# Column scales spread by a stride-0 weight read, modulation prepared later, split work re-ordered, value products in turns

## The chip, the cores and the metric

The kernel runs on one core of one Trainium2 chip. The metric is device time in microseconds (us) of one execution. Three runs of the kernel before took 2587.75, 2595.44 and 2596.06 us; their median is 2595.44 us.

## The reference

Two stacked blocks, each with two layers, on 256 tokens of width 1024, in float32.

```python
# first block, per layer
h = rms_norm(x, norm_mix_pre)
m = sigmoid(ga)*(conv(h)@wa) + sigmoid(gb)*(headnorm(retention(h))*silu(rg) @ wb) \
  + sigmoid(gc)*(headnorm(gated_linear_attention(h))*silu(gr) @ wc)
x = x + rms_norm(m @ w_out, norm_mix_post)
x = x + rms_norm((silu(h2 @ w_gate) * (h2 @ w_up)) @ w_down, norm_ffn_post)   # h2 = rms_norm(x, norm_ffn_pre)

# second block, per layer, for 256 latent tokens and 256 context tokens
mod = silu(c) @ ada_w[l] + ada_b[l]            # shift, scale and gate columns
hx  = rmsnorm(x, norm1_w) * (1 + sc1) + sh1
x   = x + g1 * (merge of conformer_conv, bidirectional mLSTM, attention with 8 heads of 64) @ w_out
x   = x + g2 * conv_ffn(rmsnorm(x, norm2_w) * (1 + sc2) + sh2)
```

`rms_norm` divides each token by the root of its mean square over the 1024 columns; `headnorm` does so in each head. In the attention, the probabilities of 64-column heads multiply values of 64 columns.

## The kernel before, in words

The kernel is bound to weights: 2-D weights stream from memory in chunks of 128x1024 float32 (512 KB), by `load` (L188) on SP's DMA queue, into five `raw` buffers. `halve` splits a chunk into a high half (`whi`, ACT, L197) and a low half (`wlo`, DVE, L199), both in a rounded float32 form that TensorE takes in one pass. Activations are split in the same way (`xh`/`xl`, `hh`/`hl`, `fah`/`fal`). `mmT` then makes 24 matmuls of 256 columns out of a chunk: high times high (L214), high times low (L218), low times high (L220). The other token-major form is L228 to L232; in the very first projection `pk`, lines 655 and 656.

The program is one long stream of such chunks with the other work laid between. A scheduler orders instructions by priority; `high_priority(offset=PRE_...)` pulls a step forward (splits, norms, `soon`), `issue_after` holds one behind another. Side work (scores, norms, convolutions) lies in generators, advanced by `tick()` after each chunk's matmuls.

The pieces that the change touches:

- **Norms.** `squares` (ACT L252, POOL or DVE sums L255/L259), a matmul with a column of ones (`st`, L273), and `rs_pair`: the -1/2 power on POOL (L281). `rs_diags` then scales the identity by the column, one 128x128 tile `dg` for each half of the tokens (DVE, L289), and `spread` (L296) multiplies a matrix of ones by it, which gives the scale on all partitions (`rsb`). `warm` puts spare matmuls into the wait.
- **Modulation.** `ada_prep` loads the two vectors `c`, each spread to 128 partitions (512 KB), on ACT's DMA queue (L357) and makes silu of them with a tanh on ACT (L361) and a DVE operation (L362). `ada_step` (L376) streams one 512 KB chunk of `ada_w` and multiplies it by the two vectors: two custom DVE operations, with sums to `mods`. There are 96 such steps. `ada_pace(every)` says how many weight chunks lie between two steps.
- **Retention and GLA.** `gn_finish` does the head norm: mean (L945, L946), centring (`on`, L947), sum of squares (L953), `rsqrt` (eight small DVE instructions, L239 to L244), scaling. `gla_scores` makes `gs` (PE, L922), and DVE L930 copies it under a mask. `ga` (ACT L860) feeds the matmul `gl` (L866).
- **Attention.** After the scores (`sc`, L1435) and their transposes (`pT`), the value products `po` (L1455) take 64 columns of values as the stationary operand. Two heads write the two 64-partition halves of one accumulator; `r` is the half, `k` the block of 128 keys (four blocks, or two for the context).
- **The end.** `down` (L214 to L220, `dn`) makes output rows in four pairs `j`; after each, `b2_residual` (L1814) adds it to `xc`, and SP writes it out (L1893).

Of the kernel before, what the change touches and what calls it, by code (L numbers as in the profile page):

```python
# [8 lines left out]
F32 = mybir.dt.float32  # L9
# [3 lines left out]
AF = mybir.ActivationFunctionType  # L13
# [89 lines left out]
class Kern:  # L103
# [87 lines left out]
    def halve(self, raw, n, after=None):  # L191

        nc = self.nc
        with self.tc.high_priority(offset=self.PRE_SPLIT):
            hi = self.p_w.tile([128, 1024], F32R, tag="whi", name=self.nm("whi"))[:, 0:n]
            lo = self.p_w.tile([128, 1024], F32R, tag="wlo", name=self.nm("wlo"))[:, 0:n]
            nc.scalar.activation(hi, raw, AF.Copy)  # L197
            with self.tc.issue_after(after.ins) if after else nullcontext():
                self.mark = nc.vector.tensor_tensor(out=lo, in0=raw, in1=hi.bitcast(F32), op=ALU.subtract)  # L199
        return hi, lo  # L200
# [63 lines left out]
    def rs_cols(self, parts, mean_ones):  # L264


        nc = self.nc
        V = nc.vector
        ps = self.aux("st")
        n = parts[0].shape[-1] // 128  # L270
        for i, p in enumerate(parts):
            for tt in range(n):
                self.small = nc.tensor.matmul(ps[:, 2 * tt : 2 * tt + 2], p[:, tt * 128 : (tt + 1) * 128], mean_ones, start=i + tt == 0, stop=i == len(parts) - 1 and tt == n - 1)  # L273
        return self.rs_diags(ps[:, 0 : 2 * n : 2])

    def rs_pair(self, x, scale):

# [3 lines left out]
        self.nc.gpsimd.tensor_tensor(out=y, in0=h, in1=self.mhalf[:, 0:n], op=ALU.pow)  # L281
        return y

    def rs_diags(self, x):

        self.rsy = y = self.rs_pair(x, 1.0)
        dg = [self.dgt() for _ in range(x.shape[-1])]
        for tt in range(len(dg)):
            self.nc.vector.tensor_scalar(dg[tt], self.ident, y[:, tt : tt + 1], None, ALU.mult)  # L289
        return dg  # L290

    def spread(self, dg):

        ps = self.aux("rsb")
        for t in range(len(dg)):
            self.small = self.nc.tensor.matmul(ps[:, t * 128 : (t + 1) * 128], self.ones, dg[t], start=True, stop=True)  # L296
        return ps[:, 0 : 128 * len(dg)]

    def warm(self, n):

# [6 lines left out]
    def setup(self, es):  # L307
# [42 lines left out]
        self.silu = c.tile([128, 2, 1024], F32, name="silu")  # L350
        self.mods = c.tile([128, 2, 48, 2], F32, name="mods")

    def ada_prep(self):
        nc = self.nc
        for s in range(2):
            v = self.silu[:, s]
            nc.scalar.dma_start(v, self.d["c2"][s : s + 1].to_broadcast([128, 1024]))  # L357
            for i in range(2):
                th = self.u("adr")
                x = v[:, 512 * i : 512 * i + 512]  # L360
                nc.scalar.activation(th, x, AF.Tanh, scale=0.5)  # L361
                nc.vector.scalar_tensor_tensor(x, th, 1.0, x, ALU.add, ALU.mult)  # L362

# [122 lines left out]
    def b1_norm(self, wname):  # L486

        A, V = self.nc.scalar, self.nc.vector  # L490
        st = {}
        hl = [(self.u("xh", F32R), self.u("xl", F32R)) for _ in range(4)]
        with self.tc.high_priority(offset=self.PRE_NORM):
            for j, (hi, lo) in enumerate(hl):
                for a in range(2):
                    sl, k = slice(a * 256, a * 256 + 256), 2 * j + a
                    A.activation(hi[:, sl], self.xc[:, k, 0:256], AF.Copy, scale=self.col(wname, k))
        with self.soon():
            for j, (hi, lo) in enumerate(hl):
                for a in range(2):  # L500
                    sl, k = slice(a * 256, a * 256 + 256), 2 * j + a
                    V.scalar_tensor_tensor(lo[:, sl], self.xc[:, k, 0:256], self.col(wname, k), hi[:, sl].bitcast(F32), ALU.mult, ALU.subtract)
        self.later("norm", self.b1_norm_rest(wname, st))
        return (*self.pairs(hl), st)

    def b1_norm_rest(self, wname, st):
        A, V = self.nc.scalar, self.nc.vector
        now = self.now
        yield from self.until(now + 1)
        with self.soon():  # L510
            parts = self.squares([self.x_pair(j) for j in range(4)])
        yield from self.until(now + self.T1)
        with self.tc.high_priority(offset=self.PRE_NORM):
            dg = self.rs_cols(parts, self.m1024)
            st["y"] = self.rsy
        xw = []
        for j in range(4):
            t = self.u("xw")
            for a in range(2):
                A.activation(t[:, a * 256 : a * 256 + 256], self.xc[:, 2 * j + a, 0:256], AF.Copy, scale=self.col(wname, 2 * j + a))  # L520
            xw.append(t)
        yield from self.until(now + self.T2)
# [12 lines left out]
        yield  # L535
# [134 lines left out]
            self.nc.tensor.transpose(ps[0:16, t * 128 : t * 128 + 128], m[t], self.ident)  # L670
        return ps[0:16, 0:256]

    def down(self, l, j, H, L, name):

        ps = self.mm("dn")
        for r, kt in ((0, 8), (8, 8), (16, 6)):
            for a in range(2):
                w = self.chunk(name, l, r * 128, kt, (2 * j + a) * 128, 128)
                self.mmT(ps[:, a * 256 : a * 256 + 256], w, H[r : r + kt], L[r : r + kt], first=r + a == 0, last=r == 16 and a == 1)
                self.tick()  # L680
        return ps
# [9 lines left out]
    def b1_layer(self, l, ahead):  # L691
# [21 lines left out]
        self.later("gla", self.gla_scores(gla))  # L713
        if l == 0:
            self.later("conv", self.b1_tables())
            self.ada_prep()
            for i in range(2):
                for nm in ("ret_gn_w", "gla_gn_w"):
                    c = self.cols(f"{nm}{i}")
                    V.tensor_scalar(c, c, 0.5, None, ALU.mult)  # L720
        else:
            self.ada_pace(8)
        gv.append(self.u("gv"))
        A.activation(gv[1], self.b1_tok(l, GV + 256, H, L), AF.Copy)
        rv = []
# [54 lines left out]
        def branch(b, j, y, gt):  # L780
# [10 lines left out]
            else:  # L791
                (V if b == 2 else G).tensor_tensor(out=macc[j], in0=macc[j], in1=gt, op=ALU.add)

        for j in range(4):
            branch(0, j, yA, gates(0, j))
        gB = [gates(1, j) for j in range(3)]
# [25 lines left out]
        first.append(self.b1_pairT(l, 256, H, L, "w_ffn_gate"))  # L822
        self.drain("norm")
        H, L = st["HL"]
        self.ada_pace(2, 1)
        for j in range(B1_FF // 2):
            pg = first[2 * j] if j < 2 else self.b1_pairT(l, 256 * j, H, L, "w_ffn_gate")
            if j < 2:
# [53 lines left out]
    def gla_scores(self, gla):  # L882
# [11 lines left out]
        for i, h in enumerate(lv):  # L894
            if h is None:
                q, k = gq, gk
            else:
# [2 lines left out]
                c4 = cum.rearrange("p (a n m) -> p (a n) m", a=2, m=2 * h)  # L900
                e4 = e.rearrange("p (a n m) -> p (a n) m", a=2, m=2 * h)
                V.tensor_tensor(out=e4, in0=c4, in1=c4[:, :, h - 1 : h].to_broadcast([128, 2 * n, 2 * h]), op=ALU.subtract)
                V.scalar_tensor_tensor(e, e, -1.0, e, ALU.mult, ALU.min)
                A.activation(e, e, AF.Exp, scale=1.0 / 16)
                q, k = self.u("ql"), self.u("kl")
                V.tensor_tensor(out=q, in0=gq, in1=e, op=ALU.mult)
                G.tensor_tensor(out=k, in0=gk, in1=e, op=ALU.mult)
# [25 lines left out]
    def gn_finish(self, o_tok, wname, sg, center, name, res):  # L933
# [5 lines left out]
        for tt in range(2):  # L939
# [13 lines left out]
            V.tensor_reduce(v, sq.rearrange("p (h v) -> p h v", h=4), AX.X, ALU.add)  # L953
            V.tensor_scalar(v, v, 1.0 / 128, EPS, ALU.mult, ALU.add)
            y = self.sm("rsh", 4)
            self.rsqrt(y, v, 4)
            V.tensor_tensor(out=c3, in0=c3, in1=y[:, :, None].to_broadcast([128, 4, 128]), op=ALU.mult)
            on.append(c)
            yield
# [453 lines left out]
    def attention(self, qT, kv, out, pool, scores):  # L1413
# [4 lines left out]
        for i in range(4):  # L1418
# [30 lines left out]
                turn(*b)  # L1449
                yield  # L1450
            po = self.aux("po")
            for r in range(2):
                for k in range(nk):
                    vt = kv[k // 2][1]
                    T.matmul(po[64 * r : 64 * r + 64, 0:256], vt[:, (k % 2) * 128 + 64 * c : (k % 2) * 128 + 64 * c + 64], pT[r][k // 2][:, (k % 2) * 256 : (k % 2) * 256 + 256], start=k == 0, stop=k == nk - 1)  # L1455
            A.activation(hi, po[:, 0:256], AF.Copy)
# [1 line left out]

    def soon(self):
        return self.tc.high_priority(offset=self.PRE_SOON)  # L1460

    def dgt(self):
        return self.p_s.tile([128, 128], F32, tag="dg", name=self.nm("dg"), bufs=4)

    def mlstm_gates(self, l, s, ps, need_rows):

# [398 lines left out]
    def b2_ffn(self, l):  # L1865
# [21 lines left out]
                self.ffn_conv(l, f, ps, c[-1], views)  # L1887
            act.append(self.hl(self.ffn_gate(*c), "fa", 0.5, self.gu if j < 3 else self.u))
        H, L = self.pairs(act)
        for j in range(4):  # L1890
            ps = self.down(l, j, H, L, "ffn_w_down_2")
            self.b2_residual(l, 0, j, ps, 40)
            self.nc.sync.dma_start(self.d["outT"][256 * j : 256 * j + 256].rearrange("(k p) t -> p k t", p=128), self.x_pair(j))  # L1893

    def b2_ffn_both(self, l, latent, prep, ahead):

# [86 lines left out]
    def b2(self):  # L1983
# [7 lines left out]
            self.b2_prep(1)  # L1991

        if "b1" not in self.parts:
            self.ada_prep()
            self.b2_start()
        self.b2_mixer(0, lambda s: (self.drain("norm"), ahead("x", 0, 1, 0, (2, 4), True)) if s == 0 else ahead("c", 0, 1, 1, (3, 5), True))
# [8 lines left out]
    def run(self, es):  # L2005
        tc, nc = self.tc, self.nc
        self.setup(es)
        with tc.high_priority(offset=5000):

            nc.scalar.activation(self.sm("warm", 2), self.m1024, AF.Copy)  # L2010
        if "b1" in self.parts:
# [129 lines left out]
```

## Time and profile before

| | |
|---|---|
| median of three runs | 2595.44 us |
| profiled execution, its time | 2584.17 us |
| profiled execution, its span (first to last instruction) | 2581.5 us |
| TensorE busy (PE) | 2524.3 us, 98% |
| weight loads (PEld, beside PE) | 2319.6 us, 90% |
| VectorE (DVE) | 1949.0 us, 75% |
| ScalarE (ACT) | 1282.6 us, 50% |
| GpSimd (POOL) | 144.4 us, 6% |
| mean granted TensorE clock | 0.997 |

The share of an engine is a mean over 2581.5 us; stages differ. In a timeline row the first number is the start, the second the time from the first start to the last end of the merged instructions (xN), and the bracket the idle time ahead of it and what ended it. Two successive instructions of an engine overlap by some 0.08 us in the records, so a row of one lasts longer than it takes in a stream.

### The profile page before, as it was taken

The numbers are of one execution on the slowest core, as the hardware profiler recorded it, in microseconds if no ns is written. First come the engines' busy times: TensorE is split into PE (matmuls) and PEld (weight loads), VectorE is DVE, ScalarE is ACT, GpSimd is POOL, SyncE is SP. The second block draws the span as 40 slices with busy tenths as digits, with TensorE's granted clock in tenths as the row PEclk, the third lists the DMA queues.
The fourth block names the chain that finished last, engine by engine and source line by source line (L and its number), as shares of the span: only waits on it lengthen the run. The fifth ranks groups of instructions, "written<-read, shape, count | busy, mean of one in ns | idle before, by whom it ended". The sixth has DMA issues, their size and how long they took to land. (4 is left out here: it accounts for less than half of the span.)

```text
span 2581.5 us, 44809 instructions
## 1 busy us (share of the span) xinstructions
PE 2524.3 (98%) x18010; PEld 2319.6 (90%) x18010; DVE 1949.0 (75%) x3254; ACT 1282.6 (50%) x2003; POOL 144.4 (6%) x151
## 2 busy tenths in 40 slices
PE   7999999999999999999999999999999999999999
PEld 7999999999999999888977679988889899999999
DVE  6987799699869958876884456975677674966994
ACT  5545544553454546343444534642345644665763
POOL 0100000010100001000010110000000000000000
PEclk9999999999999999999999999999999999999999
DMA  6545488554656754322333224434336333444554
GB/s 232 172 165 180 146 266 258 188 196 149 206 177 212 263 182 168 114 90 90 107 102 111 74 107 148 167 124 141 115 127 203 136 106 121 141 131 155 178 190 148
DMA packets 116209, 405.62 MB, mean 157 GB/s; under 512 B 12817, under 2 KB 16529, under 8 KB 116001
## 3 DMA queue, kind: packets, MB, share of 16 engines
q1 hardware_dynamic: 112880, 397.96, 46.0%
q10 hardware_dynamic: 3120, 4.80, 0.5%
q8 instruction: 141, 2.31, 0.4%
q14 instruction: 68, 0.55, 0.1%
HBM read 401.66 MB, written 1.05 MB: 156 GB/s over the span
## 5 line engine op out<-in xcount | busy, mean ns | idle before, releaser
L199 DVE TENSOR_TENSOR wlo<-raw,whi 128x1024 fp32r<-128x1024 f32 (+3 forms) x674 | 816.0, 1215 | 353.9 <-ACT whi L197 352.2
L197 ACT ACTIVATE whi<-raw 128x1024 fp32r<-128x1024 f32 (+3 forms) x674 | 697.7, 1040 | 591.8 <-PE pj L220 222.3
L214 PE MATMUL pj<-hh,whi 128*128 128x256 f32 (+1 forms) x3120 | 528.8, 311 | 5.5 <-ACT whi L197 4.0
L218 PE MATMUL pj<-hh,wlo 128*128 128x256 f32 (+1 forms) x3120 | 523.5, 309 | 4.3 <-DVE wlo L199 3.7
L214 PEld LDWEIGHTS pj<-hh,whi 128*128 128x128 f32 x3120 | 437.3, 188 | 46.2 <-ACT whi L197 5.2
L218 PEld LDWEIGHTS pj<-hh,wlo 128*128 128x128 f32 x3120 | 435.6, 189 | 43.4 <-DVE wlo L199 8.1
L220 PE MATMUL pj<-hl,whi 128*128 128x256 f32 (+1 forms) x2440 | 389.0, 296 | 0.0
L220 PEld LDWEIGHTS pj<-hl,whi 128*128 128x128 f32 x2440 | 329.6, 188 | 17.5 <-issue 0.3
L376 DVE CUSTOM_DVE_ANT_0 adr<-raw,silu 128x1024 bf16<-128x1024 f32 x192 | 238.1, 1245 | 0.5
L220 PE MATMUL pj<-kc,whi 128*128 128x512 f32 (+1 forms) x680 | 151.8, 344 | 0.0
L1263 DVE SCALAR_TENSOR_TENSOR dw<-z,hw,dw 128x512 f32<-128x512 f32 (+1 forms) x240 | 135.9, 609 | 0.2
L220 PEld LDWEIGHTS pj<-kc,whi 128*128 128x128 f32 x680 | 112.2, 188 | 16.7
L1821 ACT ACTIVATE fc<-pj,vecs 128x256 f32<-128x256 f32 (+1 forms) x78 | 52.0, 667 | 113.9 <-PE pj L220 111.3
L228 PE MATMUL pk<-whi,hh 128*128 128x256 f32 (+1 forms) x512 | 88.0, 291 | 0.0
L1822 DVE SCALAR_TENSOR_TENSOR fc<-pj,vecs,fc 128x255 f32<-128x255 f32 (+1 forms) x78 | 47.4, 609 | 48.7 <-ACT fc L1821 47.9
L230 PE MATMUL pk<-wlo,hh 128*128 128x256 f32 (+1 forms) x512 | 83.7, 283 | 0.0
L218 PE MATMUL dn<-fah,wlo 128*128 128x256 f32 (+1 forms) x440 | 76.5, 301 | 0.9 <-DVE wlo L199 0.9
L214 PE MATMUL dn<-fah,whi 128*128 128x256 f32 (+1 forms) x440 | 76.7, 301 | 0.0
L220 PE MATMUL dn<-fal,whi 128*128 128x256 f32 (+1 forms) x440 | 76.5, 300 | 0.1
L228 PEld LDWEIGHTS pk<-whi,hh 128*128 128x128 f32 x512 | 72.5, 190 | 3.0 <-issue 0.7
L255 POOL TENSOR_TENSOR sq<-sq,sq 128x512 f32<-128x512 f32 x15 | 25.2, 1681 | 855.5 <-ACT sq L252 642.8
L214 PE MATMUL pj<-yh,whi 128*128 128x256 f32 (+1 forms) x384 | 71.5, 313 | 0.0
(432 smaller groups left out, 3686.2 us busy)
## 6 DMA issues: line engine op xcount, KB each, us to landing
raw<-stream SPq DMA_DIRECT2D x620, 512.0 KB, 3.6
raw<-ada_stream SPq DMA_DIRECT2D x96, 512.0 KB, 3.9
raw<-stream SPq DMA_DIRECT2D x36, 384.0 KB, 3.5
raw<-stream SPq DMA_DIRECT2D x11, 408.0 KB, 3.2
raw<-stream SPq DMA_DIRECT2D x6, 272.0 KB, 2.7
xc<-xT SPq DMA_DIRECT2D x2, 512.0 KB, 5.6
xc<-cT ACTq DMA_DIRECT2D x1, 1024.0 KB, 10.9
silu<-c ACTq DMA_DIRECT2D x2, 512.0 KB, 12.6
```

The source lines that it names most:

```text
L197: nc.scalar.activation(hi, raw, AF.Copy)
L199: self.mark = nc.vector.tensor_tensor(out=lo, in0=raw, in1=hi.bitcast(F32), op=ALU.subtract)
L214: mm(out, wh[:, k, cs], xh[k], start=first and k == 0, stop=False)
L218: mm(out, wl[:, k, cs], xh[k], start=False, stop=False)
L220: mm(out, wh[:, k, cs], xl[k], start=False, stop=last and k == kt - 1)
L228: mm(out, xh[k], wh[:, k, :], start=first and k == 0, stop=False)
L230: mm(out, xh[k], wl[:, k, :], start=False, stop=False)
L255: nc.gpsimd.tensor_tensor(out=sqs[0], in0=sqs[0], in1=sq, op=ALU.add)
L376: nc.vector.tensor_tensor_reduce(junk, raw, self.silu[:, s], 0.5, 0.0, ALU.mult, ALU.add, self.mods[:, l, n, s : s + 1])
L1263: V.scalar_tensor_tensor(d, src, w, d, ALU.mult, ALU.add)
L1821: A.activation(v(t), v(ps), AF.Identity, scale=w(1), bias=self.col(f"ffn_conv_b{l}", f + i))
L1822: V.scalar_tensor_tensor(v(t)[..., 1:256], v(ps)[..., 0:255], w(0), v(t)[..., 1:256], ALU.mult, ALU.add)
```

## The change

It does these things, each in the diff below:

- `spread` takes the column itself: one column is read 128 times with step 0 as the stationary operand, and the identity is the moving operand. `rs_diags`, `dg` and its buffers go (36 DVE instructions).
- Six spare matmuls stand at the start of the program.
- The squares of the first norm are issued after the last high split that was made; the low halves of `xc` lose their raised priority.
- The two loads for silu move to SP's queue, between weight chunks; the tanh part moves to just before the branch loop of layer 0's mixer.
- The pace of `ada_step`: none in the projections of mixer 1 (it was every 8 chunks), every 4 in the branch loop of both layers, every 3 in the FFN (it was every 2). Steps by weight chunk: before, 25 at chunks 90 to 138, 8 at 166 to 222 and 15 at 244 to 272; now 9 at 42 to 74, 17 at 91 to 139, 9 at 194 to 226 and 13 at 244 to 280. The 48 steps after that keep their places.
- `gn_finish` takes the -1/2 power on POOL; a minimum on DVE in the GLA decay becomes an absolute value on ACT.
- The value products run through `k` outside and `r` inside.
- The last quarter of the final output is made by halves, each with its own residual and write, the second in two pieces on two queues.

```diff
-            nc.scalar.activation(hi, raw, AF.Copy)
+            self.high = nc.scalar.activation(hi, raw, AF.Copy)
...
-    def spread(self, dg):
+    def spread(self, y):
         ps = self.aux("rsb")
-        for t in range(len(dg)):
-            self.small = self.nc.tensor.matmul(ps[:, t * 128 : (t + 1) * 128], self.ones, dg[t], start=True, stop=True)
-        return ps[:, 0 : 128 * len(dg)]
+        n = y.shape[-1]
+        for t in range(n):
+            self.small = self.nc.tensor.matmul(ps[:, t * 128 : (t + 1) * 128], y[:, t : t + 1].to_broadcast([128, 128]), self.ident, start=True, stop=True)
+        return ps[:, 0 : 128 * n]
...
+    def ada_load(self):
+        for s in range(2):
+            self.nc.sync.dma_start(self.silu[:, s], self.d["c2"][s : s + 1].to_broadcast([128, 1024]))
...
-            nc.scalar.dma_start(v, self.d["c2"][s : s + 1].to_broadcast([128, 1024]))
...
-        with self.soon():
+        with self.soon(), self.tc.issue_after(self.high.ins):
             parts = self.squares([self.x_pair(j) for j in range(4)])
...
-            self.ada_prep()
+            self.ada_load()
...
-        else:
-            self.ada_pace(8)
...
+        if l == 0:
+            self.ada_prep()
+        self.ada_pace(4, 1)
         for j in range(4):
             branch(0, j, yA, gates(0, j))
...
-        self.ada_pace(2, 1)
+        self.ada_pace(3, 1)
...
-                V.scalar_tensor_tensor(e, e, -1.0, e, ALU.mult, ALU.min)
-                A.activation(e, e, AF.Exp, scale=1.0 / 16)
+                A.activation(e, e, AF.Abs)
+                A.activation(e, e, AF.Exp, scale=-1.0 / 16)
...
-            self.rsqrt(y, v, 4)
+            nc.gpsimd.tensor_tensor(out=y, in0=v, in1=self.mhalf[:, 0:4], op=ALU.pow)
...
-            for r in range(2):
-                for k in range(nk):
+            for k in range(nk):
+                for r in range(2):
...
+        def done(a, ps):
+            k = 6 + a
+            for i in range(1 + a):
+                c = slice(256 * i // (1 + a), 256 * (i + 1) // (1 + a))
+                x = self.xc[:, k, c]
+                V.scalar_tensor_tensor(x, ps[:, c], self.mods[:, l, 40 + k, 0:1], x, ALU.mult, ALU.add)
+                (self.nc.scalar if i else self.nc.sync).dma_start(self.d["outT"][128 * k : 128 * k + 128, c], x)
+
+        self.down(l, 3, H, L, "ffn_w_down_2", done)
...
+            ps = self.aux("warm")
+            for _ in range(6):
+                nc.tensor.matmul(ps[:, 0:256], self.ones, self.one256, start=True, stop=True)
```

How the order of the engines moves, at three places. First ACT in the first projections of layer 0, before: `whi` are the splits of successive chunks, `gv` a copy of a projection, `adr` the tanh for silu, `ga` what the GLA decay's matmul waits for.

```order
L416 DMA xc<-cT 128x8x256
L197 ACTIVATE whi_443<-raw_441 128x1024
L197 ACTIVATE whi_488<-raw_486 128x1024
L709 ACTIVATE gv_416<-pk_152,rs_234 128x256
L709 ACTIVATE gv_416<-pk_153,rs_234 128x256
L357 DMA silu<-c 128x1024 x2
L197 ACTIVATE whi_525<-raw_523 128x1024
L361 ACTIVATE adr_422<-silu 128x512
L361 ACTIVATE adr_425<-silu 128x512
L361 ACTIVATE adr_429<-silu 128x512
L361 ACTIVATE adr_432<-silu 128x512
L860 ACTIVATE ga_471<-ga_472 16x256
```

The same place now (line numbers of the changed file, other buffer numbers):

```order
L413 DMA xc<-cT 128x8x256
L197 ACTIVATE whi_434<-raw_432 128x1024
L197 ACTIVATE whi_479<-raw_477 128x1024
L715 ACTIVATE gv_419<-pk_159,rs_241 128x256
L715 ACTIVATE gv_419<-pk_160,rs_241 128x256
L197 ACTIVATE whi_516<-raw_514 128x1024
L867 ACTIVATE ga_462<-ga_463 16x256
L197 ACTIVATE whi_565<-raw_563 128x1024
```

The four `adr` and the two loads are gone from between the split of the eleventh chunk and `ga`; the loads stand on SP's queue now, one ahead of that chunk's predecessor (`raw_477`) and one ahead of the next (`raw_563`).

Second, DVE in mixer 1 where the retention's head norm meets the GLA scores, before: `ro` is the retention's output, `on` its centred copy, `rsh` and `rst` the steps of the root, `gs` the scores, `cy` and `yal` the convolution branch.

```order
L243 SCALAR_TENSOR_TENSOR rst_7232<-rst_7232,var_7228 128x4
L769 TENSOR_TENSOR cy_7139<-pj_7146,cy_7139 128x512
L244 SCALAR_TENSOR_TENSOR rsh_7231<-rst_7232,rsh_7231 128x4
L946 TENSOR_SCALAR mu_7282<-mu_7282 128x4
L199 TENSOR_TENSOR wlo_7411<-raw_7408,whi_7410 128x1024
L242 TENSOR_TENSOR rst_7232<-rsh_7231 128x4
L579 TENSOR_TENSOR yal_7247<-cy_7139,yah_7246 128x512
L243 SCALAR_TENSOR_TENSOR rst_7232<-rst_7232,var_7228 128x4
L947 TENSOR_TENSOR on_7281<-ro_7178,mu_7282 128x512
L244 SCALAR_TENSOR_TENSOR rsh_7231<-rst_7232,rsh_7231 128x4
L930 COPY_PREDICATED S_6271<-Am_125,gs_7305 128x2x128
```

And now:

```order
L952 TENSOR_REDUCE mu_7204<-ro_7111 128x4
L964 TENSOR_TENSOR on_7154<-on_7154,rsh_7164 128x512
L773 TENSOR_TENSOR cy_7072<-pj_7079,cy_7072 128x512
L953 TENSOR_SCALAR mu_7204<-mu_7204 128x4
L199 TENSOR_TENSOR wlo_7317<-raw_7314,whi_7316 128x1024
L575 TENSOR_TENSOR yal_7169<-cy_7072,yah_7168 128x512
L954 TENSOR_TENSOR on_7203<-ro_7111,mu_7204 128x512
L937 COPY_PREDICATED S_6219<-Am_132,gs_7216 128x2x128
```

The small steps are gone, and the scaling of the first half (`on_7154`, L964) now stands ahead of `cy`, the split and the centring of the second half (`on_7203`).

Third, PE at the first value products of the attention, before: `pT` are the transposed probabilities of the two heads, `vt` the values, x2 are two key blocks in one row.

```order
L1455 MATMUL po_15752<-pT_15532,vt_13152 64x256 x2
L1455 MATMUL po_15752<-pT_15533,vt_13120 64x256 x2
L1455 MATMUL po_15752<-pT_15534,vt_13152 64x256 x2
L1455 MATMUL po_15752<-pT_15535,vt_13120 64x256 x2
```

And now:

```order
L218 MATMUL pj_15604<-hh_10909,wlo_15608 128x512
L1462 MATMUL po_15623<-pT_15403,vt_13031 64x256
L1462 MATMUL po_15623<-pT_15405,vt_13031 64x256
L1462 MATMUL po_15623<-pT_15403,vt_13031 64x256
L1462 MATMUL po_15623<-pT_15405,vt_13031 64x256
L1462 MATMUL po_15623<-pT_15404,vt_12999 64x256
L1462 MATMUL po_15623<-pT_15406,vt_12999 64x256
L1462 MATMUL po_15623<-pT_15404,vt_12999 64x256
L1462 MATMUL po_15623<-pT_15406,vt_12999 64x256
```

The eight matmuls of a group are the same; four of one half and then four of the other have become one of each in turn.

## Rows read from the trace of the kernel before

**Rows 1.** The page, busy time of each engine over the span.

```profile
PE 2524.3 (98%) x18010; PEld 2319.6 (90%) x18010; DVE 1949.0 (75%) x3254; ACT 1282.6 (50%) x2003; POOL 144.4 (6%) x151
```

**Rows 2.** The waits of PE: who for whom, us in total, times, longest.

```profile
PE gl L866 <- ACT ga L860: 3.7, 1, 3.7
...
PE rsb L296 <- DVE dg L289: 2.4, 5, 0.5
```

**Rows 3.** Windows: stretch, its length; busy time by engine, clock, DMA share, GB/s.

```profile
46.05:52.50 6.45, 6.45 (x25) 5.61 (x26) 5.97 (x11) 4.54 (x6) 0.00 (x0) 0.51 0.39 129
128.00:160.00 32.00, 31.39 (x272) 30.43 (x270) 30.99 (x72) 14.27 (x19) 1.72 (x3) 1.00 0.38 132
160.00:245.00 85.00, 85.00 (x758) 84.50 (x756) 60.23 (x85) 41.54 (x50) 9.36 (x6) 1.00 0.54 183
305.00:487.00 182.00, 175.47 (x1478) 170.91 (x1477) 156.78 (x209) 81.98 (x99) 1.80 (x1) 1.00 0.76 250
640.00:745.00 105.00, 104.70 (x922) 103.67 (x921) 82.84 (x120) 51.40 (x63) 11.13 (x7) 1.00 0.62 206
783.00:960.00 177.00, 173.80 (x1487) 172.09 (x1486) 145.39 (x202) 91.09 (x120) 3.29 (x3) 1.00 0.69 230
```

**Rows 4.** Timeline of PE, the first products, 7 to 24 us.

```profile
13.12 0.82 PE L655 MATMUL pk<-whi,xh 128*128 128x272 f32 x2 [2.56 <-ACT whi L197]
...
16.50 0.43 PE L656 MATMUL pk<-wlo,xh 128*128 128x272 f32 x1
...
18.49 0.29 PE L656 MATMUL pk<-wlo,xh 128*128 128x272 f32 x1
...
22.79 1.07 PE L218 MATMUL pj<-xh,wlo 128*128 128x256 f32 x8
23.69 0.50 PE L220 MATMUL pj<-xl,whi 128*128 128x256 f32 x3
```

**Rows 5.** Timeline of ACT, 7 to 14 us.

```profile
10.12 2.17 ACT L252 ACTIVATE sq<-xc 128x512 f32<-128x512 f32 x4
```

**Rows 6.** Timeline of ACT and its queue, 29 to 47 us.

```profile
42.54 1.15 ACT L361 ACTIVATE adr<-silu 128x512 f32<-128x512 f32 x2 [9.26 <-DMA silu<-c]
...
45.88 1.04 ACT L197 ACTIVATE whi<-raw 128x1024 fp32r<-128x1024 f32 x1
```

**Rows 7.** Timeline of PE, 46 to 50 us.

```profile
48.02 1.22 PE L228 MATMUL pk<-whi,hh 128*128 128x256 f32 x4
```

**Rows 8.** Timeline of DVE in FFN 0, 384 to 400 us.

```profile
387.28 1.22 DVE L199 TENSOR_TENSOR wlo<-raw,whi 128x1024 fp32r<-128x1024 f32 x1
388.41 1.22 DVE L376 CUSTOM_DVE_ANT_0 adr<-raw,silu 128x1024 bf16<-128x1024 f32 x1
...
389.56 1.22 DVE L199 TENSOR_TENSOR wlo<-raw,whi 128x1024 fp32r<-128x1024 f32 x1
390.70 0.68 DVE L834 TENSOR_TENSOR s<-pj,s 128x512 f32<-128x512 f32 x1
```

**Rows 9.** Timeline of PE, 605 to 616 us.

```profile
608.04 1.10 PE L220 MATMUL pj<-hl,whi 128*128 128x256 f32 x8
...
613.37 2.04 PE L922 MATMUL gs<-ql,kl 64*128 64x128 f32 x8 [2.47 <-DVE rsh L244]
```

**Rows 10.** Timeline of DVE, 609 to 615 us.

```profile
612.54 0.68 DVE L947 TENSOR_TENSOR on<-ro,mu 128x512 f32<-128x512 f32 x1
```

**Rows 11.** Timeline of PE, attention, 1420.5 to 1425.2 us.

```profile
1421.00 2.86 PE L1455 MATMUL po<-pT,vt 128*64 128x256 f32 x16
1423.79 1.14 PE L1435 MATMUL sc<-kT,qT 64*128 64x256 f32 x8
```

**Rows 12.** The same of 1424 to 1500 us, the groups of two key blocks.

```profile
1452.60 1.09 PE L1455 MATMUL po<-pT,vt 128*64 128x256 f32 x8
```

**Rows 13.** Line 1455 over the whole span: the length of one record.

```profile
L1455 PE MATMUL po<-pT,vt x160: 379/379/431, 1421.0 to 2347.5; 128*64 128x256 f32 x160
```

**Rows 14.** Timeline of all engines, 2575 us to the end.

```profile
2577.63 0.88 DVE L1814 SCALAR_TENSOR_TENSOR xc<-dn,mods,xc 128x256 f32<-128x256 f32 x2 [7.68 <-PE dn L220]
```

More of the change, by code (lines that the diff above doesn't have):

```diff
@@ L273, in rs_cols @@
                 self.small = nc.tensor.matmul(ps[:, 2 * tt : 2 * tt + 2], p[:, tt * 128 : (tt + 1) * 128], mean_ones, start=i + tt == 0, stop=i == len(parts) - 1 and tt == n - 1)
-        return self.rs_diags(ps[:, 0 : 2 * n : 2])
+        self.rsy = self.rs_pair(ps[:, 0 : 2 * n : 2], 1.0)
+        return self.rsy
     def rs_pair(self, x, scale):
@@ L282, in rs_pair @@
         return y
[L284 to L290, printed above, removed]
-    def spread(self, dg):
+    def spread(self, y):
         ps = self.aux("rsb")
-        for t in range(len(dg)):
-            self.small = self.nc.tensor.matmul(ps[:, t * 128 : (t + 1) * 128], self.ones, dg[t], start=True, stop=True)
-        return ps[:, 0 : 128 * len(dg)]
+        n = y.shape[-1]
+        for t in range(n):
+            self.small = self.nc.tensor.matmul(ps[:, t * 128 : (t + 1) * 128], y[:, t : t + 1].to_broadcast([128, 128]), self.ident, start=True, stop=True)
+        return ps[:, 0 : 128 * n]
     def warm(self, n):
@@ L355, in ada_prep @@
         for s in range(2):
-            v = self.silu[:, s]
-            nc.scalar.dma_start(v, self.d["c2"][s : s + 1].to_broadcast([128, 1024]))
             for i in range(2):
                 th = self.u("adr")
-                x = v[:, 512 * i : 512 * i + 512]
+                x = self.silu[:, s, 512 * i : 512 * i + 512]
                 nc.scalar.activation(th, x, AF.Tanh, scale=0.5)
@@ L497, in b1_norm @@
                     A.activation(hi[:, sl], self.xc[:, k, 0:256], AF.Copy, scale=self.col(wname, k))
-        with self.soon():
[L499 to L502, printed above, removed]
+        for j, (hi, lo) in enumerate(hl):
+            for a in range(2):
+                sl, k = slice(a * 256, a * 256 + 256), 2 * j + a
+                V.scalar_tensor_tensor(lo[:, sl], self.xc[:, k, 0:256], self.col(wname, k), hi[:, sl].bitcast(F32), ALU.mult, ALU.subtract)
         self.later("norm", self.b1_norm_rest(wname, st))
@@ L509, in b1_norm_rest @@
         yield from self.until(now + 1)
-        with self.soon():
+        with self.soon(), self.tc.issue_after(self.high.ins):
             parts = self.squares([self.x_pair(j) for j in range(4)])
@@ L671, in turned, with down @@
         return ps[0:16, 0:256]
-    def down(self, l, j, H, L, name):
+    def down(self, l, j, H, L, name, done=None):
         ps = self.mm("dn")
+        if done:
+            for a in range(2):
+                p = ps[:, a * 256 : a * 256 + 256]
+                for r, kt in ((0, 8), (8, 8), (16, 6)):
+                    w = self.chunk(name, l, r * 128, kt, (2 * j + a) * 128, 128)
+                    self.mmT(p, w, H[r : r + kt], L[r : r + kt], first=r == 0, last=r == 16)
+                    self.tick()
+                done(a, p)
+            return
         for r, kt in ((0, 8), (8, 8), (16, 6)):
@@ L1460, in soon @@
         return self.tc.high_priority(offset=self.PRE_SOON)
-    def dgt(self):
-        return self.p_s.tile([128, 128], F32, tag="dg", name=self.nm("dg"), bufs=4)
     def mlstm_gates(self, l, s, ps, need_rows):
@@ L1889, in b2_ffn @@
         H, L = self.pairs(act)
-        for j in range(4):
+        for j in range(3):
             ps = self.down(l, j, H, L, "ffn_w_down_2")
@@ L1993, in b2 @@
         if "b1" not in self.parts:
+            self.ada_load()
             self.ada_prep()
```

## The prediction

> **What bounds the kernel now.** I read the page first: PE is busy in 2524.3 of 2581.5 us [rows 1], so no more than 57 us of the span are free of TensorE, and a change that leaves its matmuls as they are can win only from these, from stretches at the lower clock, and from matmuls that run beside each other and do not yet. Then I read the waits of PE: they are small and many; one of 3.7 us for `ga` and, further on, one of 2.5 us for the GLA scores stand out, and five for `dg` make 2.4 us [rows 2, 9]. The windows then show where waits come in a body: in FFN 0 PE misses 6.5 of 182 us, in FFN 1 3.2 of 177, and DVE is busy 157 and 145 us there [rows 3]. The same view shows one stretch at a granted clock of 0.51, which is the 1.2 GHz level, right behind the wait for `ga`.
>
> **The change part by part.** The sum is made against the profiled execution (2584.17 us, of which 2581.5 are span, and 2.7 lie around it); the median of the runs is 11.3 us longer, and I take the same gain off it.
>
> *Spare matmuls, and squares behind the splits.* In the first products PE runs at the lower level: one that lasts 0.43 us in the records at 16.5 lasts 0.29 at 18.5 [rows 4]. PE also waits 2.56 us up to 13.12 for a split, and ACT does four squares from 10.12, for 2.17 us, ahead of it [rows 4, 5]. Behind the splits these 2.2 us go from that wait at most; the spare matmuls can raise the clock early. From 13.1 to 18.4 some 22 products stand about 0.23 us apart instead of 0.125, so 2.3 us can go there. Both together are at most 4.5 us; the chunks still have to arrive and be split, so I take 2.0 (0 to 4.5). If the norm, which now starts 2 us later, ends later, the `xl` products wait for nothing of it; the spread behind it does, and there products stand by to fill.
>
> *Silu later.* The loads are issued on ACT's queue behind the 1 MB of `cT`, and ACT waits 9.26 us for them, to 42.54; `ga` and the split of the next chunk stand behind the waiting instruction, so the split starts at 45.88, with no DMA named: its chunk lay there [rows 6]. PE idles 3.69 us, then does `gl` and gets to the next chunk at 48.02 [rows 2, 7], and 46.05 to 52.5 runs at 0.51 [rows 3]: 6.45 us for what takes 3.3 at the upper level. With the four tanh gone, `ga` follows its own matmul at once. What is late next is the chunk itself: 1 MB of silu now comes ahead of it in SP's queue, which is 4.2 us at the 250 GB/s of FFN 0 [rows 3]; before, the same megabyte ran beside it in another queue, so it is pushed back by less. The rows bound its landing only from above, by 45.9. I put the end of its split at 42 (43 at worst): PE, which runs dry at 42.3 now and will do so at 40, then waits 1 to 2 us instead of 3.7. I take 2.2 for the wait and 3.1 for the clock: 5.3 (1.5 if the clock falls all the same, 6.8 if the whole goes).
>
> *The pace of the modulation.* Between direct neighbours a low split takes 1.13 us of DVE, a custom operation 1.15, an elementwise one 0.60 [rows 8]. Four chunks of the FFN give PE 12 groups of eight matmuls, 0.90 us from one group's start to the next's [rows 4]: 10.8 us. DVE needs 4 x 1.13 for splits, 2 steps x 2 x 1.15, and three elementwise operations: 4.5 + 4.6 + 1.8 = 10.9. So at a step every two chunks DVE has no slack, and each hiccup reaches PE. At a step every three it is 4.5 + 3.1 + 1.8 = 9.4, 86%. Of the 6.5 + 3.2 us of idle PE, each of a dozen waits costs some 0.2 more than its idle time (the last matmul's record runs on), so 12.5 us; I let two thirds go: 8.3. The 9 steps moved to the branch stage need 9 x 2.3 = 20.7 us of DVE; from 160 to 245 it is busy 60.2 of 85 [rows 3], which makes 95%; 128 to 160 is full already (31.0 of 32), and four silu operations (2.4 us) come in at its end, where the head norms' small steps go. In mixer 1 five more steps than before in 640 to 745 make 82.8 + 11.5 of 105, 90%. At 95% I expect a few new waits: -2. So +6.3 for the whole, from -3 to +12.
>
> *Spread without `dg`.* Five waits of `rsb` for `dg` make 2.4 us [rows 2]; two `dg` take some 0.5 us of the chain ahead of each of the 18 spreads, covered by `warm` or side work in the rest. 2.0 (0 to 4). The step-0 read as a weight load is not in these rows for a column; were it slow, 36 loads would each have to be 0.2 us longer to cost 7. I take no cost: loads run beside PE.
>
> *Head norms.* PE's 2.47 us before 613.37 are put down to `rsh`, but the `on` that frees the accumulator ends at 613.2 [rows 9, 10], and that is what counts. In the new order the scaling of the first half, 0.6 us, stands ahead of `cy`, the split and this `on`, against some 0.7 us of small steps that go; so `on` ends where it did and the wait stays. 0.5 for shorter chains later (0 to 6, if the wait and the slow stretch behind it go).
>
> *Value products in turns.* Sixteen records of a group of four key blocks take 2.86 us; eight of two key blocks 1.09 us, eight of `sc`, in two row halves in turns, 1.14 [rows 11, 12]. So twice eight would be 2.0 to 2.2 if the halves ran beside each other throughout; the long group runs one half by itself first. There are eight such groups, so 8 x 0.66 to 0.86: I take 6.7 (less than nothing below). The accumulator's reader, ACT, comes earlier by as much.
>
> The Trainium skill has a rule that speaks against this one ("TensorE: Matmul & The Clock Gate", section "Part 3: Packing small matmuls — row/col tiling"): a weight load runs beside matmuls in flight only when it goes to another row group, and both column halves use all rows. The trace disagrees as far as it goes: eight records of two column halves in 1.09 us are no slower than the row halves' 1.14. By the rule the sum would be that of the rival on the turns below.
>
> *End.* The last pair takes 0.88 us on DVE behind the last matmul [rows 14]; half of it now lies under the last products: 0.4 (0 to 0.6). The absolute value on ACT costs nothing: 16 x 0.6 us on an engine busy half the time.
>
> Sum: 2.0 + 5.3 + 6.3 + 2.0 + 0.5 + 6.7 + 0.4 = 23.2, so 2561 for the profiled execution, and 2595.4 - 23.2 = **2572 us** for the median.
>
> **Rivals.**
> *Waits go whole.* If the scores' wait at 613 goes with its slow stretch (+5.5), the start gives 4.5 and FFN waits go to the last (+5): 2572 - 13 = 2559. For it: DVE has fewer instructions in all. Against: the order at 613.
>
> *Turns don't help.* If no matmul of one half may run beside one of the other, all 16 stand apart as one half's do alone. A record is 0.38 long [rows 13], so the eight of 1.09 us start 0.10 apart in two streams, and one stream's 0.20: 15 x 0.20 + 0.38 = 3.4 us instead of 2.86, so eight groups lose 4.3 where I have +6.7: 2572 + 11 = 2583. For it: the long group now, with only part beside each other. Against it the 1.09 us [rows 12].
>
> *PE's own pace takes it back.* Eight matmuls span 1.07 us at 22.79 and 1.10 at 608 [rows 4, 9]: 4.3 ns a matmul. If the two FFNs without their waits stay at the slower spacing where they had the faster, up to 1478 and 1487 x 4.3 = 6.4 us each are lost [rows 3]; if the chunk at 42 lands late besides, most of the 5.3 goes: 23.2 - 12.8 - 4 = 6: 2589. For it: both spacings stand in the trace; against: they could as well get better.
>
> *Slower: the branch stage overflows.* The 20.7 us of steps meet 24.8 us of DVE that are free from 160 to 245. If the custom operations come in ahead of splits whenever DVE is late, or if the stage needs over 4 us more than I count, the rest falls to PE. Should each of the 18 steps in the two stages hold a split by one operation, 1.15 us, and each third such wait bring a stretch at the lower level (3.2 us, as at 46 to 52 [rows 3]): 18 x 1.15 + 6 x 3.2 = 40, less the 23.2 and the 2 counted: 2610. It decides from 25.2 / 18 = 1.4 us lost a step. Against: the splits have a raised priority, and five buffers lie between.
>
> **How the numbers follow.** Forecast and its neighbourhood (2562 to 2582) 0.58; waits go whole 0.14; turns don't help 0.08; pace takes it back 0.14; overflow 0.06. About 0.3%, 8 us, can be told from no change in this kernel: under 2587.6 is faster. Forecast, first rival, the turns and a third of the pace: 0.85 faster; 0.10 within; 0.05 slower. The likeliest has 2562 to 2582 for its own; the range, 2554 to 2588, leaves out some 0.15 above and 0.04 below.
>
> **What would show it.** Right: no PE wait for `ga`, and clock 1.0 from 46 to 52; FFN 0 with under 3 us of idle PE; groups of `po` at about 2.0 us; no `rsb` wait over 0.3; the scores' wait at about 610 still there. Wrong: DVE over 97% from 160 to 245 with PE waits for `wlo` in it; `po` at 2.9 or more; PE waiting over 3 us for a split near 41; total idle of PE over 50 us.

## The result and the profile after

The changed kernel takes 2551.01 us (median of 4 runs, 2544.71 to 2555.34), the kernel before 2594.94 us (2587.75 to 2596.06): a ratio of 0.9835, 95% interval 0.9803 to 0.9866. That is 43.9 us by the medians and 38.6 us between the two profiled spans (2581.5 and 2542.9). The forecast was 2572 us with a range down to 2554: the right sign, and too little. The page after, against [rows 1]:

```profile
PE 2506.3 (99%) x18022; PEld 2309.3 (91%) x18022; DVE 1921.8 (76%) x3115; ACT 1290.3 (51%) x2017; POOL 155.9 (6%) x159
```

PE has 36.6 us free where it had 57. To see where the time came from, I marked the same points in both traces: the 5416 matmuls that read a low half of a weight chunk come about eight to a chunk, and the n-th stands at the same place of the program.

```
n-th such matmul    before     after    gain so far   stage
    0 (start)          8.1       6.8        1.2
  720 (norm, FFN 0)  310.4     303.9        6.5       first layer's mixer: +5.3
 1200                494.3     478.8       15.5       FFN 0: +9.0
 1440                591.4     575.1       16.3       +0.8
 1560                647.8     624.7       23.1       around the scores of mixer 1: +6.8
 1920                789.4     765.2       24.2       +1.1
 2400                967.4     935.8       31.6       FFN 1: +7.4
 3000               1356.9    1325.9       31.0       -0.6
 3240               1568.4    1533.8       34.6       attention, layer 0: +3.6
 4560               2245.9    2211.2       34.7       0
 4800               2362.7    2325.1       37.7       attention, layer 1: +3.0
 5400               2572.0    2533.6       38.4       +0.7
```

The windows, against [rows 3] (the columns are the same; the stretches are shifted by what was gained):

```profile
39.00:46.00 7.00, 7.00 (x61) 6.22 (x60) 3.55 (x8) 1.42 (x2) 0.00 (x0) 1.00 0.53 198
154.00:239.00 85.00, 85.00 (x758) 84.50 (x756) 76.36 (x95) 42.16 (x51) 13.73 (x8) 1.00 0.68 230
297.00:479.00 182.00, 181.17 (x1525) 180.09 (x1525) 144.38 (x185) 86.63 (x106) 2.00 (x2) 1.00 0.71 237
590.00:600.00 10.00, 9.83 (x81) 9.28 (x80) 8.40 (x16) 4.50 (x7) 1.22 (x2) 1.00 0.17 57
760.00:936.00 176.00, 175.85 (x1526) 174.97 (x1525) 143.19 (x197) 93.46 (x121) 4.85 (x4) 1.00 0.72 235
```

The FFNs have 0.8 and 0.2 us of idle PE where they had 6.5 and 3.2, and the branch stage has none with DVE at 76.4 of 85. The clock is 1.00 behind `ga` and behind the scores. In PE's waits the ones for `ga` and `dg` [rows 2] are gone; the spread now waits for POOL, five times and up to 0.7 us:

```profile
PE pj L218 <- DVE wlo L199: 2.9, 2, 1.7
PE rsb L290 <- POOL rs L282: 2.9, 5, 0.7
...
PE gs L929 <- POOL kl L914: 0.9, 1, 0.9
...
PE gs L929 <- DVE on L954: 0.3, 2, 0.2
```

The timeline of PE at the value products, against [rows 11]:

```profile
1390.07 1.95 PE L1462 MATMUL po<-pT,vt 128*64 128x256 f32 x16
```

Sixteen records take 1.95 us instead of 2.86. At the scores of mixer 1, against [rows 9], and then the end of the program, against [rows 14]. At the end PE has a wait that the kernel before did not have: the second half of the last output rows waits for the residual of the first.

```profile
594.09 1.13 PE L929 MATMUL gs<-ql,kl 64*128 64x128 f32 x8 [0.17 <-DVE on L954]
```

```profile
2531.86 1.17 PE L214 MATMUL dn<-fah,whi 128*128 128x256 f32 x8 [0.67 <-DVE xc L1904]
...
2539.65 0.61 DVE L1904 SCALAR_TENSOR_TENSOR xc<-dn,mods,xc 128x128 f32<-128x128 f32 x2 [7.93 <-PE dn L220]
```

### The profile page after: what moved, and what is told of

Its sections match the earlier page's. It is cut to its first block, busy times and chain, and to the rows that moved or that the text cites. A ratio compares the mean times of both kernels' runs of the same rounds, so it can differ in the third digit from the quotient of the medians.

```text
span 2542.9 us, 44723 instructions
## 1 busy us (share of the span) xinstructions
PE 2506.3 (99%) x18022; PEld 2309.3 (91%) x18022; DVE 1921.8 (76%) x3115; ACT 1290.3 (51%) x2017; POOL 155.9 (6%) x159
## 4 chain that ended last, share of the span: by engine, by line
PE 87%; DVE 8%; ACT 3%; issue 1%; POOL 1%; DMA 0%; ACTq 0%; DVEq 0%; POOLq 0%; SPq 0%
PE pj L214 19%; PE pj L220 19%; PE pj L218 19%; PE dn L220 4%; PE dn L218 4%; PE dn L214 4%; DVE wlo L199 2%; PE pk L228 2%; PE pk L232 2%; PE pk L230 2%; PE pv L1638 2%; DVE dw L1270 1%; PE ms L1598 1%; PE br L214 1%; PE br L218 1%
## 5 line engine op out<-in xcount | busy, mean ns | idle before, releaser
L220 PE MATMUL dn<-fal,whi 128*128 128x256 f32 (+1 forms) x440 | 76.4, 300 | 0.1
```

The lines of the kernel that those rows point to most:

```text
L220: mm(out, wh[:, k, cs], xl[k], start=False, stop=last and k == kt - 1)
```

## The experiments

All spans below are of one profiled execution each. Since they scatter by some 10 us for one and the same kernel (the last experiment but one), the verdicts rest on stages, read between the marks of the table above, and on waits.

**The paces of before in the changed kernel.**

```diff
+        else:
+            self.ada_pace(8)
...
-        self.ada_pace(4, 1)
...
-        self.ada_pace(3, 1)
+        self.ada_pace(2, 1)
```

> The changed kernel with the modulation's paces of the kernel before (every 8 chunks in mixer 1, none of its own in the branch loops, every 2 in the FFNs). Theory: the paces are worth 17 us in the two FFNs and 7 at the scores' wait in mixer 1, so it is 22 to 26 us slower than the changed kernel, with PE idle of some 6 us in FFN 0 and 3 in FFN 1, and a PE wait of about 2 us at the second gs of mixer 1. Rival, that shorter work on DVE elsewhere (norms, head norms) emptied it: 8 us slower at most, and no wait at gs.

Measured: 2563.64 us median (ratio to before 0.989, 0.9856 to 0.9923), span 2554.5, so 11.6 to 12.6 us slower than the changed kernel. FFN 0 takes 182.7 us instead of 174.9, FFN 1 176.4 instead of 170.6, the stretch around the scores 52.4 instead of 49.6, and the start was 3.5 us shorter in this execution. The waits are back, in FFN 0 over 300 to 484 us:

```profile
300.00:484.00 184.00, 177.88 (x1475) 172.59 (x1474) 155.70 (x210) 83.14 (x101) 3.39 (x3) 1.00 0.76 252
```

6.1 us idle and DVE at 156 again, as forecast. The waits come from the paces. Of the 22 to 26 us expected, half showed: the scores got back 2.8 us and not 7 (the next run), the two FFNs 13.6 and not 17, in part because FFN 0 ran with a shorter spacing of PE's matmuls (see the repeated profiles below), and the start was shorter.

**Only mixer 1's pace put back.**

```diff
+        else:
+            self.ada_pace(8)
...
+        if l == 0:
-        self.ada_pace(4, 1)
+            self.ada_pace(4, 1)
```

> The changed kernel with the pace of every 8 chunks put back into mixer 1 alone (the branch loop of layer 1 without a pace of its own). Theory, that one modulation step of 2.3 us on DVE some 20 us ahead made PE wait at the second gs: the wait comes back at 1.5 to 2.5 us with a stretch at the lower clock behind it, 4 to 7 us slower in mixer 1 and nothing elsewhere. Rival, that the head norm's small steps made it (they are still gone here): no wait over 0.5 us, within 1 us of the changed kernel.

Measured: 2549.84 us median, span 2545.6. The stretch around the scores takes 52.4 us instead of 49.6, and PE waits there:

```profile
593.59 1.13 PE L932 MATMUL gs<-ql,kl 64*128 64x128 f32 x8 [1.37 <-DVE on L957]
```

```profile
590.00:600.00 10.00, 8.63 (x56) 8.08 (x56) 8.44 (x16) 4.35 (x7) 1.01 (x1) 0.83 0.21 60
```

The wait (1.37 of 2.47 us) and the lower clock (0.83 in the window) are back by the modulation step alone, with 2.8 of the 6.8 us. That is less than the 4 to 7 us expected; what the head norm's root adds is tested below.

**Only the paces changed in the kernel before.**

```diff
-        else:
-            self.ada_pace(8)
...
+        self.ada_pace(4, 1)
         for j in range(4):
             branch(0, j, yA, gates(0, j))
...
-        self.ada_pace(2, 1)
+        self.ada_pace(3, 1)
```

> The kernel before with the new paces alone (every 4 in both branch loops, every 3 in the FFNs, none in mixer 1's projections). Theory: 22 to 25 us faster than before: 17 in the two FFNs, up to 7 in mixer 1 (a wait of under 1 us at gs, although the small steps of the root are still on DVE), nothing or -1 in the branch loops. Rival, that the branch stage had room only because the other edits emptied DVE: waits of PE for wlo between 160 and 245 us, and 3 to 10 us of the gain lost there.

Measured: 2565.28 us median, ratio to before 0.9899 (0.9865 to 0.9932), span 2559.6: 21.9 us off the span by three changed lines alone. FFN 0 takes 170.7 us (before 183.9), FFN 1 175.3 (178.0), the scores' stretch 50.7 (56.4). The branch stage gives nothing back: at mark 720 it stands 0.8 us ahead of before, and with DVE busy 77.3 of 85 us from 160 to 245 PE has no wait there. Its DVE needs none of the other edits.

**Value products by halves.**

```diff
-            for k in range(nk):
-                for r in range(2):
+            for r in range(2):
+                for k in range(nk):
```

> The changed kernel with the value products half by half again. Theory: groups of sixteen records take 2.86 us again instead of about 1.9, eight groups, so 7 to 8 us slower, all of it in the two attention stages. Rival, that the stages' gain came from the spread of the norms in them: under 2 us slower.

Measured: 2548.96 us median, span 2542.7: by the times, nothing. By the stages, attention takes 211.6 instead of 207.9 us (marks 3000 to 3240) and 117.7 instead of 113.9 (4560 to 4800): 7.5 us slower, as forecast. In this execution the start was 2 us and FFN 0 5.1 us shorter, with not one edit there.

```profile
1382.49 2.86 PE L1462 MATMUL po<-pT,vt 128*64 128x256 f32 x16
```

**The root in small steps on DVE.**

```diff
-            nc.gpsimd.tensor_tensor(out=y, in0=v, in1=self.mhalf[:, 0:4], op=ALU.pow)
+            self.rsqrt(y, v, 4)
```

> The changed kernel with the head norm's root in small steps on DVE again. Theory, that the modulation step made the wait at the second gs of mixer 1: the wait stays under 1 us, the time within 2 us. Rival, that the root on POOL removed it: PE waits 1.5 us or more there, 4 to 7 us slower.

Measured: span 2546.2. Around the scores 51.1 us instead of 49.6; the scores do not wait, a later transpose does, for 1.1 us. The rival is out as the sole cause; the root's steps are worth 1.5 us there.

**Diagonals again.** `rs_diags` and the old `spread` put back, as in the diff of the change.

> The changed kernel with the scaled identities dg again, a matrix of ones as the stationary operand. Theory: the waits of PE at the 18 spreads grow by 0.2 to 0.5 us each where nothing stands by, 2 to 4 us slower in all. Rival, that warm matmuls and side work cover the two dg operations: within 1 us.

Measured: 2540.42 us in its one run, span 2538.5, the shortest of all. Two stages are longer than in kernels with the same spacing of PE's matmuls (see the repeated profiles below): marks 1560 to 1920 take 142.1 us against 140.5 in the changed kernel, and 4560 to 5040 take 201.9 against 199.2 in the next experiment's kernel. In the second, before the last FFN, PE waits for the normed tokens and falls to the lower level for a while:

```profile
2361.42 3.18 PE L214 MATMUL pj<-hh,whi 128*128 128x256 f32 x8 [0.63 <-ACT hh L1146]
```

```profile
2355.00:2375.00 20.00, 19.27 (x135) 17.67 (x135) 18.41 (x36) 15.46 (x35) 0.71 (x1) 0.91 0.32 113
```

The kernel before, which has the diagonals too, waits at the same place:

```profile
2405.35 3.38 PE L214 MATMUL pj<-hh,whi 128*128 128x256 f32 x8 [0.63 <-ACT hh L1133]
```

In the changed kernel the same eight products start without that wait, at a clock of 1.00; from the third on they stand 0.4 us apart here too:

```profile
2367.88 2.60 PE L214 MATMUL pj<-hh,whi 128*128 128x256 f32 x8
```

The first stage is another matter. Its 1.5 us are a stretch at the lower clock among spare matmuls, and the changed kernel, which has no diagonals, has the same stretch at the same place in its second profile; the diagonals' profile first, then that one:

```profile
728.00:743.00 15.00, 13.18 (x83) 11.82 (x82) 9.02 (x16) 8.22 (x17) 3.90 (x3) 0.89 0.30 97
```

```profile
735.00:750.00 15.00, 13.09 (x79) 11.40 (x79) 8.21 (x14) 7.60 (x16) 3.45 (x3) 0.89 0.27 96
```

So the diagonals cost 2.5 to 2.7 us, at one spread and not a little at each of 18; at the others the waits of `rsb` have another name only (2.4 us for `dg`, 2.9 for POOL). The rival, under 1 us, falls, though the time alone would have spoken for it.

**Silu early, on ACT's queue.**

```diff
+            self.ada_prep()
...
-        if l == 0:
-            self.ada_prep()
...
-            self.nc.sync.dma_start(self.silu[:, s]
+            self.nc.scalar.dma_start(self.silu[:, s]
```

> The changed kernel with the silu loads on ACT's queue and the tanh ahead of ga, as before. Theory: PE idles 3 to 4 us at gl again and runs a stretch at the lower clock: 4 to 6 us slower by the time that chunk 30 is reached, nothing later. Rival, that the start's other edits (spare matmuls, squares later) made the gain: under 2 us slower.

Measured: span 2544.4; 6.2 us later at mark 120 (64 us), 4.0 at 250 us. PE waits longer than before and is released at the same instant as in [rows 2, 7]:

```profile
46.06 2.07 PE L872 MATMUL gl<-ga,kc 16*128 16x256 f32 x4 [6.05 <-ACT ga L866]
```

So with silu early the start's other edits buy 2 us that PE then waits.

**The old start.**

```diff
-        with self.soon(), self.tc.issue_after(self.high.ins):
+        with self.soon():
...
-            ps = self.aux("warm")
-            for _ in range(6):
-                nc.tensor.matmul(ps[:, 0:256], self.ones, self.one256, start=True, stop=True)
```

> The changed kernel without the six spare matmuls and with the first squares not held behind the last high split. Theory: the first products run at the lower clock until about 18 us again and PE waits 2 us for a split near 13, 1 to 3 us slower by the time that the first norm's spread is reached, of which some is lost in the wait for a chunk near 41. Rival, that DMA sets the pace up to there: no difference at 50 us.

Measured: span 2547.9; 3.2 us later at mark 30 (26 us), 4.1 at mark 120 and 1.4 at mark 720. The chunk at 41 us did not set the pace, as the rival had it; the difference dies out in the next stage.

**The changed kernel itself, twice more.** No edit.

> The changed kernel itself, unchanged, profiled again. Theory, that the spacing of PE's matmuls (0.113 or 0.118 us) is settled anew in each execution: at least one of FFN 0 and FFN 1 differs by 4 to 5 us from the first profile (FFN 0 174.9 us, FFN 1 170.6 us there between the same matmuls), with as many waits as there. Rival, that the program sets it: both within 0.5 us of the first profile.

> The changed kernel itself, unchanged, profiled a third time; theories and numbers as for the second profile. FFN 0 takes either some 170 or some 175 us, and so does FFN 1; nothing lies between by the theory, unless the spacing changes inside the stage.

Measured: spans 2553.2 and 2552.6 against 2542.9. FFN 0 takes 173.9 in both (174.9 in the first), FFN 1 174.7 in both (170.6), and the end, from mark 5040 to the last mark, 131.7 in both (127.1). PE's waits are nearly the same. The timeline of PE in FFN 1, first the second profile, then the first:

```profile
840.28 1.10 PE L218 MATMUL pj<-hh,wlo 128*128 128x256 f32 x8
841.22 1.10 PE L220 MATMUL pj<-hl,whi 128*128 128x256 f32 x8
```

```profile
840.48 1.07 PE L214 MATMUL pj<-hh,whi 128*128 128x256 f32 x8
841.39 1.07 PE L218 MATMUL pj<-hh,wlo 128*128 128x256 f32 x8
```

Groups of eight start 0.94 or 0.905 us apart. In FFN 1 the first profile has 1265 matmuls spaced about 0.113 us and 170 about 0.118; the other two have 354 and 1071. One and the same program takes either spacing in a stage and mostly keeps it; the 173.9 of FFN 0, between the two lengths that the theory allows, has both inside. FFN 1 and the end make 8.7 of the 10 us between these executions. Stretches at the lower clock add to the scatter: they lie at 11.7 us in the first profile, at 279 and 740 in the second and at 34 and 969 in the third.

The second and third profile agree with each other and come from one chip, so by themselves they do not tell whether the chip or the execution chose. The four runs of the kernel with the value products by halves, all on one chip, took 2544.2, 2544.5, 2553.5 and 2554.0 us: two groups 9 us apart, which speaks for the execution, but no trace shows the spacing of each.

**The rotary tables a projection earlier.** The first remaining waits, between 56 and 72 us.

```diff
             self.b1_masks()
+            self.later("conv", self.b1_tables())
...
-            self.later("conv", self.b1_tables())
```

> The changed kernel with the rotary tables (some 30 small DVE operations, loaded and computed beside the first projections) begun one projection earlier. Theory, that the four waits of PE between 56 and 72 us (5 us in all) come from DVE, where these operations stand among the GLA decay's and the splits: two or more of the waits shrink and the stage to chunk 30 is 1 to 4 us shorter. Rival, that the waits follow ACT's loads of function tables in the decay: no change there beyond 1 us. The whole time is then not told from the changed kernel's by its runs alone, whose executions lie 10 us apart.

Measured: 2552.47 us median, span 2548.2, at mark 240 (chunk 30) 0.4 us and at mark 480 0.2 us later than the changed kernel, where 1 to 4 us less were expected. The waits after 50 us are gone; one of 4.5 us stands ahead of them.

```profile
PE pk L230 <- DVE wlo L199: 5.1, 2, 4.5
```

The waits are DVE's, as the theory has it, but they only move: there is no better version in this.

## Why the prediction was too small

Step by step, in profiled us: what was forecast, and what the stages show.

- **FFN pace and branch stage: +6.3 forecast, +16.4 measured.** This is the step that failed, in its size. I priced a dozen waits at their idle time and 0.2 us each, and let a third stay (9.7 and 12 x 0.2 make 12.1 and not the 12.5 that I wrote, which changes little). Counted in the trace, the starts of PE's matmuls in FFN 0 stand over 0.2 us apart at 64 places before and 18 after, in FFN 1 at 35 and 19. Taking 0.115 us off each gap for the matmul that runs in it, they cost 16.0 and 3.0 us, and 7.7 and 2.3: 18.4 us go, where I let 8.3 go. The idle time that went (8.7 of the 9.7 us of [rows 3]) is only half of that: the record of the last matmul covers a part of the gap, and the first gap behind it is 0.22 us. Thirty stops went where I counted a dozen waits and let eight of them go, and each had cost some 0.3 us beyond its idle time where I had 0.2. Nearly all went, since DVE at 9.4 of 10.8 us has slack for them. The spacing took some 4 us back in FFN 0 (113 of its matmuls at the shorter one, where 1062 had been) and gave some 2 in FFN 1. The -2 for the branch stage was wrong: DVE was filled to 76.4 of 85 us, 90% where I had 95%, and no split came late; the paces alone in the kernel before lose nothing there either.

- **Head norms and scores: +0.5 forecast, +7.6 measured in mixer 1 (6.8 around the scores).** My step was "`on` ends where it did and the wait stays", from the order of the ten instructions ahead of it. That order was right and too short: what made `on` late was a queue on DVE from 25 us earlier. There stood a modulation step, which the new pace takes out of the projections:

```profile
586.90 1.23 DVE L376 CUSTOM_DVE_ANT_0 adr<-raw,silu 128x1024 bf16<-128x1024 f32 x1
...
589.18 1.21 DVE L376 CUSTOM_DVE_ANT_0 adr<-raw,silu 128x1024 bf16<-128x1024 f32 x1
```

  DVE of the kernel before then has no pause until 607 (in the timeline; 10.00 of 10 us busy from 590 to 600), and that pause, 0.7 us, is itself a wait for ACT, which squares the late centred copy of the first half. The new one stands idle three times in the same part, 0.4 to 1.0 us. The paces alone take 5.7 of the 6.8 us (the third experiment), the other edits alone 4.0 (the first), the root on POOL 1.5 (the fifth): each relieves DVE enough to cut most of one wait, and with it the slow stretch behind it, so the parts do not add up. This was my first rival, "waits go whole", for the scores and the FFNs. I gave it 0.14 and argued against it from the order; at 2559 even that rival was too small, for it priced the FFNs by idle time as well.

- **Start and silu: +7.3 forecast, +6.6 measured** at mark 120, 6.5 at mark 720. The chunk that I feared late did not hold PE at all: PE reached `gl` at 39.2 us and went on with products at 40.2 without a wait. Instead there are 4.6 us of waits between 56 and 72 us (1.0 in the kernel before), most of them for a low split on DVE; the last experiment ties them to the rotary tables' work there. The spare matmuls did not keep the clock up in the first profile, which runs at the lower level from 11.7 to 15.1 us; in the second and third no such stretch lies there. The two parts need each other: undone one by one they cost 6.2 and 4.1 us at mark 120.

- **Value products: +6.7 forecast, about +7.5 measured**, by the stages of the changed kernel with and without it. The rule of the Trainium skill ("TensorE: Matmul & The Clock Gate", section "Part 3: Packing small matmuls — row/col tiling") that a weight load runs beside matmuls only for another row group does not decide here: the trace disagrees, two column halves over the same 128 rows run beside each other in turns, 1.95 us for sixteen.

- **Spread: +2.0 forecast, about 2.5 measured**, right in size by luck, for it is not where I had it. The five waits of [rows 2] did not go: they are for POOL's power now, up to 0.7 us where I expected none over 0.3. What went is one wait of PE for `hh` in the last norm with its slow stretch.

- **Own pace of PE.** Real, a rival that I had right in kind; but it differs between executions of one program. Between the first profiles of the two kernels it was against us in FFN 0 and, by some 1 us, from mark 4800 to 5040, and for us in FFN 1 and, by some 1 us, from 1560 to 1920.

- **End: +0.4 forecast, -0.3 measured.** From the start of the last DVE operations to the span's end it is 3.25 us (2539.65 to 2542.9) where it was 3.87: +0.6, as the prediction has it. But the halves bring the new wait of PE at 2531.86, which its term left out; with its gap it costs 0.8. From mark 5040 to the end the changed kernel takes 131.3 us and the kernel before 131.0, at the same spacing.

Of the signs that the prediction named for being right, the ones for `ga`, FFN 0 and `po` came true; the ones for `rsb` and for the scores' wait did not. The spans differ by 38.6 us, against 23.2 forecast; the parts above, some read from other runs, add up to about 40. The medians lie 43.9 us apart, 5 more than the profiles, within the scatter of the executions.

## What to carry to other kernels

Price a stall of TensorE by the starts of its matmuls, not by idle time: here a stop cost twice the idle time that the profile showed. Where an engine runs at 100% in a stage, its lateness at one wait comes from everything queued since it last stood idle, so look back to its last real pause before saying that a wait stays. And when executions of one kernel scatter by more than an edit is worth, compare stages between marks; the edit of the value products moved the time by nothing and its own two stages by 7.5 us. Even a stage can mislead by a stretch at the lower clock (1.5 us at one norm here), so look for the same stretch in a repeated profile of the unchanged program.

## What the runs showed of the hardware

- Back-to-back matmuls of 256 columns, each with its weight load, run at about 0.113 or 0.118 us apart at a granted clock of 1.00, and one program took either in different profiles: FFN 1 170.6 or 174.7 us, the end from mark 5040 to the last mark 127.1 or 131.7. What sets it stays open; no run here forced the one or the other.
- Matmuls of two column halves given half by half ran one half alone for the first 0.9 us, then both beside each other, then the other half alone: 2.86 us for sixteen records; in turns 1.95.
- A weight load whose source is one column read 128 times with step 0 takes as long as one of a whole tile (190 ns against 192 before):

```profile
L290 PEld LDWEIGHTS rsb<-mats,rs x72: 185/190/192, 18.6 to 2364.8; 128*128 128x128 f32 x72
```
